# One decoder layer on one core: a 64-byte padding tile ahead of the activations in SBUF is left out

## The chip, the core and the metric

The kernel runs on one core of a Trainium2 chip. Its time is the device time of an execution in microseconds, and the figure compared is the median of several executions. A profile of one execution shows TensorE (PE, with its weight loads as PEld), VectorE (DVE), ScalarE (ACT), GpSimd (POOL), and the queue that issues most DMAs (SP).

## The reference

One layer of a hybrid decoder: two mixers side by side (differential attention and chunked retention) share an input and an output projection, and a gated MLP with a short causal convolution follows. 16 meta tokens stand ahead of 256 tokens; all is float32.

```python
u = rmsnorm(h, attn_norm) * vmask
proj = u @ w_in                              # 2048 -> 6144
aq, ak, av, rq, rk, rv, rg = jnp.split(proj, SPLITS, axis=-1)
ya = rmsnorm(diff_attention(aq, ak, av, lam, slopes, valid), attn_subln) * (1.0 - lam_init)
yr = rmsnorm(retention(rq, rk, rv, log_g), ret_norm) * silu(rg)
h = h + concat([ya, yr]) @ w_out             # 2048 -> 2048
u = rmsnorm(h, ffn_norm) * vmask
g = u @ w_gate                               # 2048 -> 5632
gc = causal_conv3(g, conv_w)
h = h + (silu(gc) * (u @ w_up)) @ w_down     # 5632 -> 2048
out = rmsnorm(h, final_norm)[:, CHUNK:]
```

## The kernel before

Every weight is used once, so the kernel is a stream over 212 chunks of 1 MB: 48 for the input projection (4 of them as `w_first`), 16 for `w_out`, 44 pairs for gate and up, 44 for `w_down`. `load` brings a chunk into `raw` by a DMA on SP, and `prep` (L118 to L131) splits each half of it into two parts of TensorE's fp32r type: ScalarE copies it into `whi` (L127), VectorE subtracts that from the original into `wlo` (L128). The activations are split in the same way into a high and a low part, and a product is three matmuls per 128 rows: high by high, high by low, low by high.

Four products follow one another on TensorE, each with a shape of its own:

- Input projection, `gemm` (L332 to L334): the weights are the stationary operand, `x` is the moving one, 258 or 272 columns. The attention and retention tasks are slipped in between.
- `w_out`, `gemm_q` on `ys` (L340 to L342): weights stationary, `ys` moving, 260, 256 and 258 columns. `ys` is the mixers' output, one row of `GW` = 544 float32 (2,176 bytes) for each of 16 steps k; the columns read begin at 28, 32 and 30 of that row (112, 128 and 120 bytes).
- Gate and up, on `g`, the normed input of the MLP, in the same layout as `ys`: `gemm_q` again for the gate (the same three lines), and `gemm_t` for the up product (L353, 512 columns that begin at byte 128 of a row; L355 or L352, 256 columns).
- Down, `down` (L709 to L711): here the activations are stationary. `fhi` and `flo` hold the MLP's 5,632 inner values as 44 rows of 256 tokens (1,024 bytes each); a matmul loads 128 of them (512 bytes) and streams 512 columns of `whi` or `wlo`. At the very end 72 matmuls of 256 columns (tile `oe`) take the place of 36 of 512.

A tile scheduler orders the instructions of each engine when the program is built. SBUF is laid out by pools, in the order in which they are opened: constants, `big`, the weights' `wts`, then `small` (statistics of a few bytes, each in a slot of 32 bytes or more), and above it the pools of the phases. The tile `spad`, [128, 16] float32, is 64 bytes in each partition and the first of `small`. Nothing reads it. In the built program the first bytes of a partition's tiles stand so:

| tile | first byte | past a multiple of 512 |
|---|---|---|
| `x` and later `g` (two tiles each, pool `big`) | 27,136 and 45,568 | 0 and 0 |
| `whi`, `wlo` (three buffers each) | 104,960 to 125,440 | 0 |
| `spad` | 129,536 | 0 |
| `ys`, later `fhi` | 130,624 | 64 |
| `flo` | 175,680 | 64 |

Of the kernel before, what the change touches and what calls it, by code (L numbers as in the profile page):

```python
# [10 lines left out]
F32 = mybir.dt.float32  # L11
# [8 lines left out]
P = 128  # L20
# [59 lines left out]
def trunk_kernel(ctx, tc, a, out):  # L80
    nc = tc.nc
    V, S, PE = nc.vector, nc.scalar, nc.tensor
# [2 lines left out]
    big = ctx.enter_context(tc.tile_pool(name="big", bufs=1))  # L85
    wp = ctx.enter_context(tc.tile_pool(name="wts", bufs=1))
    sp = ctx.enter_context(tc.tile_pool(name="small", bufs=2))
    spad = sp.tile([P, 16], F32, name="spad", bufs=1)
    V.memset(spad, 0.0)
    dp = ctx.enter_context(tc.tile_pool(name="dram", bufs=1, space=bass.MemoryType.DRAM))  # L90

    xs = [big.tile([P, 2, HK, TW], F32R, tag=f"act{i}", name=f"x{i}") for i in range(2)]
# [759 lines left out]
def build(arrs):  # L852
    import concourse.bacc as _bacc
    import concourse.tile as _tile
    from concourse import mybir as _mybir

    nc = _bacc.Bacc("TRN2", target_bir_lowering=False, num_devices=1)
    arrays, args = {}, {}
    for name, v in arrs.items():
        arrays[f"in_{name}_dram"] = v  # L860
        args[name] = nc.dram_tensor(f"in_{name}_dram", v.shape, _mybir.dt.from_np(v.dtype),
                                    kind="ExternalInput").ap()
    o = nc.dram_tensor("out_0_dram", (SEQ, D), _mybir.dt.from_np(np.dtype("float32")),
                       kind="ExternalOutput").ap()
    with _tile.TileContext(nc, schedule_with_timeline_sim=True) as tc:
        trunk_kernel(tc, args, o)
    return nc, arrays
# [8 lines left out]
```

## Time and profile before

| | |
|---|---|
| median of 3 executions | 1178.18 us (1177.35 to 1180.27) |
| the profiled execution | 1177.78 us, of which the span from first to last instruction is 1176.0 us |
| granted TensorE clock | 0.998 |
| PE busy, PEld busy | 1162.5 us (99%), 1079.7 us (92%) |
| DVE busy, ACT busy | 813.7 us (69%), 560.1 us (48%) |
| DMA | 224.42 MB, mean 191 GB/s |

A matmul's duration in the profile includes the time in which its results drain, which overlaps the next matmul; what a matmul costs on a busy TensorE is the distance from its start to the next start, called its pitch here. A row of the timeline begins with the start in us and the duration in us; an "x2" merges two instructions that follow each other. A row of a tile's view has the durations in ns as least/median/most.

### The profile page before, as it was taken

The page shows a single profiled execution, that of the slowest core. Times are in us where ns is not written, and L with a number is a line of the kernel's source. Part 1 is how long each engine was busy: PE and PEld are TensorE (multiplying, and loading weights), DVE is VectorE, ACT ScalarE, POOL GpSimd, SP SyncE. Part 2 cuts the span into 40 slices and gives each one's busy share as a digit, 9 for nine tenths or more (in the row PEclk, how much of TensorE's full clock was granted, in tenths as well). Part 3 has the DMA queues.
Part 4 walks back from the last instruction along what each step waited for, and adds up shares of the span by engine and source line. Part 5 has one row for each costly group of instructions (what it writes and reads, how often), then busy time and mean ns, then how long its engine had stood idle before and what let it go on. Part 6 is the DMA issues. An engine that isn't in the chain of part 4 may idle for free.

```text
span 1176.0 us, 20164 instructions
## 1 busy us (share of the span) xinstructions
PE 1162.5 (99%) x8039; PEld 1079.7 (92%) x8039; DVE 813.7 (69%) x1528; ACT 560.1 (48%) x922; POOL 3.7 (0%) x23
## 2 busy tenths in 40 slices
PE   9999999999999999999999999999999999999997
PEld 7999999999999999999999999999999888888886
DVE  7888887766677778777777777767777645454544
ACT  7666665443345444444444444444444434343442
POOL 0000000000000000000000000000000000000000
PEclk9999999999999999999999999999999999999999
DMA  8644545465557786555555555555555655555552
GB/s 300 210 157 163 186 149 182 160 191 177 179 184 232 228 268 222 179 182 190 198 183 180 188 197 189 180 184 195 196 179 183 225 198 182 181 192 198 181 182 105
DMA packets 76525, 224.42 MB, mean 191 GB/s; under 512 B 41362, under 2 KB 48954, under 8 KB 51472
## 3 DMA queue, kind: packets, MB, share of 16 engines
q1 hardware_dynamic: 76144, 221.96, 55.7%
q8 instruction: 63, 1.03, 0.3%
q0 software_dynamic: 144, 1.05, 0.2%
q14 instruction: 30, 0.25, 0.1%
q10 hardware_dynamic: 144, 0.14, 0.0%
HBM read 216.57 MB, written 6.55 MB: 190 GB/s over the span
## 4 chain that ended last, share of the span: by engine, by line
PE 94%; DMA 3%; DVE 1%; issue 0%; ACT 0%; SPq 0%; DVEq 0%; ACTq 0%
PE mm L353 14%; PE mm L340 10%; PE mm L342 10%; PE mm L341 9%; PE mm L332 7%; PE mm L333 7%; PE mm L334 7%; PE o L709 7%; PE o L711 7%; PE o L710 7%; PE mm L355 7%; DMA raw<-in_w_in_dram 2%; PE po L461 1%; PE ro L518 1%; DMA rvt<-rhv 1%; DMA raw<-in_w_first_dram 1%
## 5 line engine op out<-in xcount | busy, mean ns | idle before, releaser
L128 DVE TENSOR_TENSOR wlo<-raw,whi 128x1024 fp32r<-128x1024 f32 x381 | 466.4, 1224 | 278.9 <-ACT whi L127 272.5
L127 ACT CAST whi<-raw 128x1024 fp32r<-128x1024 f32 x381 | 399.9, 1050 | 472.4 <-PE o L711 132.5
L353 PE MATMUL mm<-g,whi 128*128 128x512 f32 x704 | 249.1, 392 | 0.0
L332 PE MATMUL mm<-x,whi 128*128 128x272 f32 (+1 forms) x688 | 198.8, 289 | 0.0
L340 PE MATMUL mm<-g,whi 128*128 128x260 f32 x704 | 198.7, 282 | 0.0
L333 PE MATMUL mm<-x,whi 128*128 128x272 f32 (+1 forms) x688 | 198.5, 289 | 0.0
L334 PE MATMUL mm<-x,wlo 128*128 128x272 f32 (+1 forms) x688 | 197.1, 287 | 1.4 <-DVE wlo L128 1.4
L342 PE MATMUL mm<-g,wlo 128*128 128x258 f32 x704 | 198.1, 281 | 0.0
L341 PE MATMUL mm<-g,whi 128*128 128x256 f32 x704 | 194.9, 277 | 0.0
L355 PE MATMUL mm<-g,wlo 128*128 128x256 f32 x660 | 185.1, 281 | 0.0
L353 PEld LDWEIGHTS mm<-g,whi 128*128 128x128 f32 x704 | 132.2, 188 | 25.9
L341 PEld LDWEIGHTS mm<-g,whi 128*128 128x128 f32 x704 | 133.5, 190 | 1.9
L340 PEld LDWEIGHTS mm<-g,whi 128*128 128x128 f32 x704 | 132.1, 188 | 0.0
L342 PEld LDWEIGHTS mm<-g,wlo 128*128 128x128 f32 x704 | 132.0, 187 | 0.0
L711 PE MATMUL o<-whi,flo 128*128 128x512 f32 x334 | 131.6, 394 | 0.0
L710 PE MATMUL o<-wlo,fhi 128*128 128x512 f32 x334 | 131.6, 394 | 0.0
L334 PEld LDWEIGHTS mm<-x,wlo 128*128 128x128 f32 x688 | 129.6, 189 | 1.7 <-DVE wlo L128 1.6
L333 PEld LDWEIGHTS mm<-x,whi 128*128 128x128 f32 x688 | 129.7, 189 | 0.0
L332 PEld LDWEIGHTS mm<-x,whi 128*128 128x128 f32 x688 | 129.7, 188 | 0.0
L355 PEld LDWEIGHTS mm<-g,wlo 128*128 128x128 f32 x660 | 124.3, 188 | 0.0
L709 PE MATMUL o<-whi,fhi 128*128 128x512 f32 x334 | 118.9, 394 | 0.0
L711 PEld LDWEIGHTS o<-whi,flo 128*128 128x128 f32 x334 | 62.5, 187 | 15.4
(244 smaller groups left out, 1372.7 us busy)
## 6 DMA issues: line engine op xcount, KB each, us to landing
raw<-in_w_in_dram SPq DMA_DIRECT2D x44, 1024.0 KB
raw<-in_w_gate_dram SPq DMA_DIRECT2D x44, 1024.0 KB
raw<-in_w_up_dram SPq DMA_DIRECT2D x44, 1024.0 KB
raw<-in_w_down_dram SPq DMA_DIRECT2D x44, 1024.0 KB
raw<-in_w_out_dram SPq DMA_DIRECT2D x16, 1024.0 KB
raw<-in_w_first_dram SPq DMA_DIRECT2D x6, 512.0 KB
xres<-in_x_dram SPq DMA_DIRECT2D x16, 129.0 KB
hd<-hb SPq DMA_DIRECT2D x64, 32.0 KB
```

The lines of the kernel that those rows point to most:

```text
L127: S.copy(out=hi, in_=src)
L128: V.tensor_tensor(out=lo, in0=src, in1=hi.bitcast(F32), op=ALU.subtract)
L332: PE.matmul(ps[:, :n], wh, xh, start=(k == 0), stop=False)
L333: PE.matmul(ps[:, :n], wh, xl, start=False, stop=False)
L334: PE.matmul(ps[:, :n], wl, xh, start=False, stop=(k == KT - 1))
L340: PE.matmul(ps[:, :NQ + 2], wh, src.cols(k, GO - 2, GL), start=(k == 0), stop=False)
L341: PE.matmul(ps[:, 4:NQ + 2], wh, src.cols(k, GL, GW), start=False, stop=False)
L342: PE.matmul(ps[:, 2:NQ + 2], wl, src.hi(k), start=False, stop=(k == KT - 1))
L353: PE.matmul(ps, wh, src.cols(k, GO + 2, GW), start=(k == 0), stop=(k == KT - 1))
L355: PE.matmul(ps[:, :SEQ], wl, src.cols(k, GO + 2, GL), start=False, stop=False)
L710: PE.matmul(o, ah, wl, start=False, stop=False)
L711: PE.matmul(o, al, wh, start=False, stop=stop and kk == 1)
```

## The change

`spad` and the instruction that clears it are left out. Every tile of the pools that lie above it moves down by 64 bytes in each partition: the rest of `small`, `ys` (to 130,560), `fhi` (130,560), `flo` (175,616), and all working tiles of the attention, retention, and MLP phases (`q2`, `k2`, `at`, `vt`, `fg`, `fs` and others). 130,560 and 175,616 are multiples of 512. The constants, `x`, `g`, `klz`, `htok`, `raw`, `whi` and `wlo` lie below and stay. The order of the instructions on each engine is the same but for the one that is gone; all lines below it have numbers smaller by 2.

```diff
     sp = ctx.enter_context(tc.tile_pool(name="small", bufs=2))
-    spad = sp.tile([P, 16], F32, name="spad", bufs=1)
-    V.memset(spad, 0.0)
     dp = ctx.enter_context(tc.tile_pool(name="dram", bufs=1, space=bass.MemoryType.DRAM))
```

## The prediction

> **What bounds the kernel now.** I read the page first (busy shares, then the chain that ended last), then the busy time by stretch, then who waits for TensorE, and last single rows of the timeline in the two stages that the moved tiles feed.
>
> ```profile
> PE 1162.5 (99%) x8039; PEld 1079.7 (92%) x8039; DVE 813.7 (69%) x1528; ACT 560.1 (48%) x922; POOL 3.7 (0%) x23
> PE 94%; DMA 3%; DVE 1%; issue 0%; ACT 0%; SPq 0%; DVEq 0%; ACTq 0%
> ```
>
> TensorE is busy for 99% of the span, and 94% of the chain that ended last is its own work. By stretch (length, then busy time and count of PE, PEld, DVE, ACT, POOL, the granted clock, DMA):
>
> ```profile
> 350.00:424.00 74.00, 74.00 (x622) 74.00 (x621) 55.84 (x107) 37.56 (x68) 0.00 (x0) 1.00 0.79 239
> 925.00:1148.00 223.00, 223.00 (x957) 178.73 (x956) 108.11 (x98) 90.31 (x96) 0.65 (x1) 1.00 0.55 191
> 500.00:900.00 400.00, 400.00 (x2843) 375.62 (x2842) 290.11 (x464) 183.01 (x285) 0.00 (x0) 1.00 0.54 187
> ```
>
> The first stretch is `w_out`, the second the down product, the third gate and up. TensorE never pauses in them, at full clock, while DVE and ACT have room. So in these stages nothing but the pitch of the matmuls makes time, and a change of addresses can only act through that pitch.
>
> Does the pitch depend on the address at all? The trace has a controlled pair: `gemm_q` runs with the same three shapes on `ys` and on `g`, both rows of 2,176 bytes, with the weights in the same buffers. Only the first byte differs: `ys` begins 64 past a multiple of 512, `g` on one. From the timeline, the first and last of 49 rows on `ys`, then on `g` (48 pitches, so 16 steps of three, each time):
>
> ```profile
> 399.80 0.28 PE L340 MATMUL mm<-ys,whi 128*128 128x260 f32 x1
> ...
> 405.53 0.28 PE L340 MATMUL mm<-ys,whi 128*128 128x260 f32 x1
> ```
>
> ```profile
> 606.97 0.28 PE L340 MATMUL mm<-g,whi 128*128 128x260 f32 x1
> ...
> 612.63 0.39 PE L353 MATMUL mm<-g,whi 128*128 128x512 f32 x1
> 612.87 0.28 PE L355 MATMUL mm<-g,wlo 128*128 128x256 f32 x1
> ```
>
> On `ys` the 48 take 5.73 us (358.1 ns for three), on `g` 5.66 us (353.8 ns). And the durations by tile:
>
> ```profile
> L340 PE MATMUL mm<-ys,whi x256: 277/284/291, 334.9 to 426.3; 128*128 128x260 f32 x128
> L341 PE MATMUL mm<-ys,whi x256: 276/279/287, 335.1 to 426.4; 128*128 128x256 f32 x128
> L340 PE MATMUL mm<-g,whi x704: 277/282/470, 426.7 to 915.8; 128*128 128x260 f32 x176
> L341 PE MATMUL mm<-g,whi x704: 274/278/281, 426.8 to 915.9; 128*128 128x256 f32 x176
> ```
>
> A row of 2,176 bytes is 4 x 512 + 128, so from k to k+1 the first byte steps by 128 in the 512, and each tile visits four positions. On `ys` the spread is 276 to 287 ns for one shape, on `g` 274 to 281. The timeline shows that on `ys` every fourth step is the slow one:
>
> ```profile
> 400.51 0.29 PE L340 MATMUL mm<-ys,whi 128*128 128x260 f32 x1
> 400.64 0.29 PE L341 MATMUL mm<-ys,whi 128*128 128x256 f32 x1
> ...
> 401.94 0.29 PE L340 MATMUL mm<-ys,whi 128*128 128x260 f32 x1
> 402.07 0.29 PE L341 MATMUL mm<-ys,whi 128*128 128x256 f32 x1
> ```
>
> So the address does act, through its place within 512 bytes, by one to three per cent of a matmul.
>
> **The change part by part.** *The instruction that goes.*
>
> ```profile
> 0.85 0.07 DVE L89 MEMSET spad<- 128x16 f32 x1
> 0.90 0.17 DVE L160 MEMSET ones<- 128x128 f32 x1
> 1.62 3.11 PE L178 MATMUL psx<-warm 128*128 128x512 bf16 x7 [1.62 <-DVE warm L166]
> 5.02 0.81 PE L231 MATMUL mm<-x,whi 128*128 128x258 f32 x4 [0.28 <-ACT x L213]
> ```
>
> The clears behind it start 0.05 us sooner (0.85 for 0.90), and with them the seven warm-up matmuls, which wait for `warm`. The first real matmul waits for ACT at 5.02, so this is covered: 0. No DMA is added, removed or moved past another, and no wait changes.
>
> *`w_out`.* After the change `ys` begins on a multiple of 512, with the layout of `g`: the 16 steps read from exactly the positions within 512 that the gate product reads today. I take the pitch of `g`: 16 chunks x (5.66 - 5.73) us = -1.1 us. Bounds: 0, if the difference comes from what runs beside it, and -1.2 us (to the rounding of these rows).
>
> *The down product.* Between these two rows of the chain of waits lie 80 repeats of 2.80 us, twelve matmuls each:
>
> ```profile
> 924.65 0.47 PE o L709 x2
> 1148.65 0.47 PE o L709 x2
> ```
>
> That is 224.00 us for 960 matmuls of 512 columns, 233.3 ns each. In all there are 1,020 of these (334 of each line, and 18 from the last tiles) and 72 of 256 columns. What changes is the stationary side: each slice of `fhi` and `flo` begins 64 past a multiple of 512 now, and on it afterwards. The moving side (`whi`, `wlo`) stays on multiples of 512. No down row has both on 512; the nearest is the up product, with weights on 512 and `g` 0, 128, 256 or 384 past it:
>
> ```profile
> L353 PE MATMUL mm<-g,whi x704: 388/393/398, 432.0 to 921.5; 128*128 128x512 f32 x176
> L709 PE MATMUL o<-whi,fhi x334: 388/394/398, 921.7 to 1157.8; 128*128 128x512 f32 x167
> L709 PEld LDWEIGHTS o<-whi,fhi x334: 187/187/192, 921.5 to 1157.6; 128*128 128x128 f32 x167
> L353 PEld LDWEIGHTS mm<-g,whi x704: 187/188/190, 431.9 to 921.3; 128*128 128x128 f32 x176
> 601.39 0.39 PE L353 MATMUL mm<-g,whi 128*128 128x512 f32 x1
> ```
>
> From 601.39 to the gate's first row at 606.97 the 16 pairs of 512 and 256 columns take 5.58 us, 348.8 ns a pair. At the down product's rate per column (233.3 / 512) a pair would take 350.0 ns. So both sides on 512 run 0.35% faster per column, 0.8 ns of 233.3, and x 1,020 that is -0.8 us. By the median durations of L353 and L709 (393 and 394) it would be -1.0 us; I take -0.9. The fast bound is the least duration of L709, 388 for 394: -6 ns x 1,020 = -6.1 us. The slow bound is what 64 bytes do to the moving side on `ys`, 287 for 279 in L341: +8 ns x 1,020 = +8.2 us; in the middle lies the most of L709, 398 for 394, +4.1 us. The weight load itself takes 187 ns at the median from an address 64 past (L709), as long as the 188 ns from one on 512 (L353), so its own duration gives no gain.
>
> *The rest.* The attention matmuls that read moved tiles are short and few:
>
> ```profile
> L461 PE MATMUL po<-vt,at x96: 270/272/303, 78.9 to 206.5; 100*86 100x128 f32 x48, 86*86 86x128 f32 x48
> L411 PE MATMUL sc<-k,q x48: 207/252/371, 55.6 to 193.5; 128*86 128x100 f32 x16, 128*86 128x186 f32 x16, 128*86 128x272 f32 x16
> ```
>
> These 144, and as many again for what the rows leave out, at the 2 ns by which the medians of L340 above differ, are 0.6 us either way; I take 0. The moved tiles that DVE and ACT write and read are not on the path: in the rows below the idle time of TensorE ahead of its groups (behind the bar, second) is 0.0 in the stages at issue.
>
> ```profile
> L711 PE MATMUL o<-whi,flo 128*128 128x512 f32 x334 | 131.6, 394 | 0.0
> L340 PE MATMUL mm<-ys,whi 128*128 128x260 f32 x256 | 72.3, 284 | 0.0
> ```
>
> The sum: 0 - 1.1 - 0.9 = -2.0 us. The profiled execution took 1177.78 us, 1.78 beyond its span, and 0.40 below the median of 1178.18, so it would take 1175.8 and the median 1176.2 us. A measurement of this kernel tells about 0.3%, 3.5 us, from no change; -2.0 is inside.
>
> [...]
>
> **The rivals.** *A: the down product falls toward its floor.* The weight load for the next matmul starts as the present one starts, so both streams run side by side, and the present 64 bytes between them could be a poor distance. For it: at the same distance of 64 bytes the pitch isn't fixed by the shape, since 256 columns there take
>
> ```profile
> 1163.07 0.28 PE L710 MATMUL oe<-wlo,fhi 128*128 128x256 f32 x1
> ...
> 1164.43 0.28 PE L710 MATMUL oe<-tailt,fhi 128*128 128x256 f32 x1
> ```
>
> 1.36 us for twelve, 113.3 ns, so twice that, 226.7, is possible for 512, 6.7 ns below today's. Against it: L353 reaches 388 only at its least. Half to all of the fast bound gives -3 to -6.1 us, with `w_out` -4.1 to -7.2: 1171 to 1174 us, 1172.5 in the middle.
>
> *B: the two streams collide when both begin on the same byte of 512.* They start together, and reading the same part of SBUF at once could hold one of them up. For it: those 113.3 ns, at a distance of 64, are below what 256 columns cost in the up product with both sides at distances of 0 to 384 (a third of 348.8, 116 ns, by columns). Price: from +4 ns (the most of L709 over its median) to +8 ns (L341 on `ys`) a matmul, +4.1 to +8.2 us, less `w_out`'s 1.1; it decides from +4.5 ns a matmul, where the sum passes +3.5 us. Its middle, +6 ns, gives +6.1 - 1.1 = +5.0 us, 1183 us. Against it: L353, whose every fourth step has both on 512, has no slow group (398 at most, as L709 has).
>
> *C: nothing happens.* `ys` is slower for what runs beside it (DMA at 0.79 there, 0.54 in gate and up), and the distance in the down product is indifferent: 1178.2 us. Against it stands the slow fourth step, which no neighbour's work would repeat so evenly.
>
> **How the numbers follow.** The forecast 0.36, C 0.10, A 0.34, B 0.20. The forecast is ahead of A because it has a stage with both sides on multiples of 128 and the weights on 512, timed over hundreds of matmuls, where A has only the short ones of the end. The first two fall within 0.3%: 0.46; A is faster, 0.34; B is slower, 0.20. The range reaches from 1170.5 (all of A's -7.2, and the 0.6 us of the short matmuls) to 1182 (B at +4 ns with no gain in `w_out`); the upper half of B is left out. The forecast's own range is 1174.7 to 1178.2, where no change begins.
>
> **What would show it.** In the profile after, 48 `gemm_q` pitches on `ys` take 5.66 us and no fourth step stands out; if 5.73 stays, C is right. Twelve matmuls of the down product take 2.79 us; 2.72 would be A, 2.85 or more B. Gate, up and input projection must keep their pitches. I am wrong if the pitch depends on something other than the place within 512 bytes.

## The result, and the profile after

The median went from 1178.18 us to 1172.66 us (seven executions each, 1170.49 to 1174.53 after), a ratio of 0.9946 with a 95% interval of 0.9931 to 0.9961: 5.5 us faster, about half a per cent. The profiled execution has a span of 1170.9 us, 5.1 us less. Times below leave out one slow execution, of the kernel called rows128 here, which took 1255.13 us at a granted clock of 0.85.

From the page of the kernel after, the busy times, the matmuls of 512 columns of the up product, and the largest matmul group of the down product (line numbers are smaller by 2):

```profile
PE 1156.8 (99%) x8039; PEld 1081.4 (92%) x8039; DVE 813.6 (69%) x1527; ACT 560.7 (48%) x922; POOL 3.7 (0%) x23
L351 PE MATMUL mm<-g,whi 128*128 128x512 f32 x704 | 249.1, 392 | 0.0
L709 PE MATMUL o<-whi,flo 128*128 128x512 f32 x334 | 130.0, 389 | 0.0
```

TensorE has the same matmuls and is still busy for 99%; the mean of a down matmul fell from 394 to 389 ns, that of the up product stayed at 392. The chain of waits after: the first, second and last of rows that stand twelve matmuls apart, as quoted for before:

```profile
925.85 0.45 PE o L707 x2
928.57 0.45 PE o L707 x2
...
1143.45 0.45 PE o L707 x2
```

From 925.85 to 1143.45 are 217.60 us for 80 repeats, 2.72 us for twelve, against 2.80. The pitch is 226.7 ns, 6.67 ns less than before. By tile, for the stationary side (its load first), the end of the down product (the row before, of L709, stands ahead of the row after, of L707), and `ys`:

```profile
L707 PEld LDWEIGHTS o<-whi,fhi x334: 187/188/192, 922.7 to 1152.4; 128*128 128x128 f32 x167
L707 PE MATMUL o<-whi,fhi x334: 389/389/396, 922.9 to 1152.6; 128*128 128x512 f32 x167
L709 PE MATMUL oe<-whi,fhi x12: 276/281/283, 1151.5 to 1165.6; 128*128 128x256 f32 x12
L707 PE MATMUL oe<-whi,fhi x12: 278/283/287, 1146.2 to 1160.3; 128*128 128x256 f32 x12
L338 PE MATMUL mm<-ys,whi x256: 277/282/285, 337.4 to 427.6; 128*128 128x260 f32 x128
L339 PE MATMUL mm<-ys,whi x256: 274/278/290, 337.5 to 427.7; 128*128 128x256 f32 x128
```

The weight load takes as long as before (188 for 187 ns at the median): nothing about the load itself is quicker. The stream `whi` has not moved by a byte. Yet the matmul that streams it while the load runs is shorter (389 for 394 ns at the median), so it is the two together that cost less. The 256-column matmuls of the end went the other way, from 281 to 283 ns at the median. On `ys` the slow fourth step is gone (285 at the most in L338, for 291), and 48 pitches, first and last row:

```profile
399.68 0.28 PE L338 MATMUL mm<-ys,whi 128*128 128x260 f32 x1
...
405.33 0.28 PE L338 MATMUL mm<-ys,whi 128*128 128x260 f32 x1
```

take 5.65 us, close to the 5.66 on `g`. Stage lengths, each from the start of a stage's first matmul to that of the next stage's, in us:

| stage | before, three profiles | after, three profiles | difference of the means |
|---|---|---|---|
| input projection, attention, retention | 333.31, 334.05, 333.12 | 335.78, 334.86, 335.65 | +1.94 |
| `w_out` | 91.74, 91.76, 91.76 | 90.57, 90.57, 90.57 | -1.18 |
| gate and up | 495.01, 495.01, 495.01 | 494.99, 494.99, 494.99 | -0.02 |
| down, to the last matmul's start | 246.14, 246.14, 246.14 | 239.80, 239.80, 239.80 | -6.34 |

The sum is -5.60 us, what the medians say. The last three stages repeat to 0.02 us; the first does not, and part of its growth is the granted clock, as the last experiments show. (The second and third profile of each kernel come from the runs below.)

### The profile page after: what moved, and what is told of

The parts are those of the page before. It is cut to its first block, busy times and chain, and to the rows that moved or that the text cites. A ratio compares the mean times of both kernels' runs of the same rounds, so it can differ in the third digit from the quotient of the medians.

```text
span 1170.9 us, 20163 instructions
## 1 busy us (share of the span) xinstructions
PE 1156.8 (99%) x8039; PEld 1081.4 (92%) x8039; DVE 813.6 (69%) x1527; ACT 560.7 (48%) x922; POOL 3.7 (0%) x23
## 4 chain that ended last, share of the span: by engine, by line
PE 93%; DMA 5%; DVE 2%; SPq 0%; issue 0%; ACT 0%; DVEq 0%; ACTq 0%
PE mm L351 14%; PE mm L340 10%; PE mm L338 10%; PE mm L339 9%; PE mm L353 7%; PE o L707 7%; PE o L709 7%; PE o L708 7%; PE mm L331 6%; PE mm L330 6%; PE mm L332 6%; DMA raw<-in_w_first_dram 2%; DMA rvt<-rhv 1%; PE po L459 1%; DMA raw<-in_w_in_dram 1%; PE ro L516 1%
## 5 line engine op out<-in xcount | busy, mean ns | idle before, releaser
L338 PE MATMUL mm<-g,whi 128*128 128x260 f32 x704 | 198.7, 282 | 0.0
L353 PE MATMUL mm<-g,wlo 128*128 128x256 f32 x660 | 185.1, 281 | 0.0
L338 PEld LDWEIGHTS mm<-g,whi 128*128 128x128 f32 x704 | 132.1, 188 | 0.0
L709 PE MATMUL o<-whi,flo 128*128 128x512 f32 x334 | 130.0, 389 | 0.0
L353 PEld LDWEIGHTS mm<-g,wlo 128*128 128x128 f32 x660 | 124.3, 188 | 0.0
L707 PE MATMUL o<-whi,fhi 128*128 128x512 f32 x334 | 117.1, 389 | 0.0
L709 PEld LDWEIGHTS o<-whi,flo 128*128 128x128 f32 x334 | 62.7, 188 | 13.0
```

Source lines behind the costliest of these rows:

```text
L338: PE.matmul(ps[:, :NQ + 2], wh, src.cols(k, GO - 2, GL), start=(k == 0), stop=False)
L353: PE.matmul(ps[:, :SEQ], wl, src.cols(k, GO + 2, GL), start=False, stop=False)
L709: PE.matmul(o, al, wh, start=False, stop=stop and kk == 1)
```

## The experiments

All kernels are the changed one with the edit shown. "48 on ys" and "twelve" stand for those pitches, read as above.

**Which part gives the time: padding back ahead of `ys` alone, or of `fhi` and `flo` alone.**

```diff
+        ypad = yp.tile([P, 16], F32, name="ypad")
+        V.memset(ypad, 0.0)
         ys = Packed([yp.tile([P, KT, GW], F32R, name="ys")])
```

> 64 bytes of padding stand ahead of ys alone: ys and the attention and retention tiles are back at their places of before, fhi and flo stay on multiples of 512. Theory (the gain is the down product's stationary side): twelve down matmuls take 2.72 us, 48 matmuls on ys 5.73 us, and the time is 6 us under before, ratio 0.9945 to 0.9955. Rival (the gain comes from ys and the tiles beside it): down at 2.80 us per twelve, ratio 0.998 or more.

```diff
+        fpad = fp.tile([P, 16], F32, name="fpad")
+        V.memset(fpad, 0.0)
         fhi = fp.tile([P, NF, SEQ], F32R, name="fhi")
```

> 64 bytes of padding stand ahead of fhi and flo alone; ys is on a multiple of 512. Theory (down's stationary side): twelve down matmuls take 2.80 us again, 48 matmuls on ys 5.66 us, and only w_out's 1.2 us of the gain is left, ratio 0.998 to 1.001. Rival (ys and its neighbours carry the gain): 1172 to 1174 us, ratio 0.995 to 0.997.

With `ys` at its old place: 1172.48 us beside 1178.92, ratio 0.9943 (0.9929 to 0.9958). `w_out` takes 91.76 us, as before, down 239.80, as after. With `fhi` and `flo` at theirs: 1177.73 us, ratio 0.9985 (0.9973 to 0.9998), `w_out` 90.57, down 246.14. From the chain of waits and by tile, the second kernel:

```profile
927.79 0.47 PE o L709 x2
930.59 0.47 PE o L709 x2
L709 PE MATMUL o<-whi,fhi x334: 387/395/398, 924.8 to 1161.0; 128*128 128x512 f32 x167
```

Twelve take 2.80 us again. So 64 bytes under the stationary side of the down product carry the gain, and `w_out` its 1.2 us. Both runs go the theory's way, and the rival's numbers fit neither.

**Distance or absolute place: padding ahead of the weights too.** Now `whi` and `wlo` lie 64 past a multiple of 512 as well as `ys`, `fhi` and `flo`; only `g` and `x` stay.

```diff
     wp = ctx.enter_context(tc.tile_pool(name="wts", bufs=1))
+    wpad = wp.tile([P, 16], F32, name="wpad")
+    V.memset(wpad, 0.0)
```

> 64 bytes of padding stand ahead of the weights: raw, whi, wlo, ys, fhi and flo all begin 64 past a multiple of 512, x and g on one. Theory (the distance between the streamed and the loaded operand within 512 bytes decides): twelve down matmuls at distance 0 take 2.72 us, ys against whi at the old distance of the gate product 5.66 us for 48, and gate, up and input projection change their pitch, since their distance is now 64 less. Rival (the absolute place decides, a loaded slice must begin on 512): down at 2.80 us, ys at 5.73 us, and gate and up slower by the 3% of a 512-column matmul, some 7 us.

1172.46 us, ratio 0.9944 (0.9927 to 0.9962). From the chain of waits:

```profile
925.55 0.45 PE o L709 x2
928.27 0.45 PE o L709 x2
```

```profile
L340 PE MATMUL mm<-ys,whi x256: 277/282/286, 335.9 to 426.0; 128*128 128x260 f32 x128
L353 PE MATMUL mm<-g,whi x704: 389/397/398, 431.8 to 922.4; 128*128 128x512 f32 x176
```

Nothing in the down product begins on a multiple of 512, except for its last tiles, and twelve take 2.72 us. `ys` also has its good pitch, 64 past, since `whi` is too. What changed for the worse is gate and up, 496.23 us for 494.99: `g` is on 512 and the weights are not (L353's median 397 for 393). So it is the distance between the loaded and the streamed operand. The price of it on gate and up was 1.2 us, far from the 7 that the rival named. The last tiles agree: `tailt` and `endt` stayed on multiples of 512 while `fhi` and `flo` lie 64 past, and twelve matmuls of 256 columns that stream `tailt` take 1.36 us here, as before the change, and 1.44 in the changed kernel (1158.45 to 1159.81, and 1158.66 to 1160.10).

**A map of the distance.** The rows of `fhi` and `flo` are put into one tile, in eight groups of six, with a gap between groups (`GAP` = 16 float32, 64 bytes; then 4, 16 bytes), so that one execution has eight distances. `ul` has one buffer for two, to make room. The diff leaves out the lines that write and read the rows through `row`.

```diff
+        fhl = fp.tile([P, 2 * NF * SEQ + 7 * GAP], F32R, name="fhl")
+        def row(lo, f, b=0, n=SEQ):
+            g = f // 6
+            s = g * (12 * SEQ + GAP) + lo * (6 if g < 7 else 2) * SEQ + f % 6 * SEQ + b
+            return fhl[:, s:s + n]
...
```

> fhi and flo lie in eight groups of six rows (the last of two), each group 64 bytes further from the last multiple of 512: 0, 64, 128 to 448, so that one run shows the down pitch at eight distances (one buffer less for the tile ul, which gate and up may feel a little). Theory (distance): 226.7 ns in the group at 0, 233.3 at 64, and a value of its own for each other distance, repeated in the four passes over the 44 rows. Rival (only a start on 512 is special): 226.7 at 0 and 233.3 in the seven others. Rival (no dependence on the place, the new pitch has another cause): one pitch in all groups.

> As the map in steps of 64, with eight groups that begin 0, 16, 32 to 112 bytes past a multiple of 512. Theory (distance decides, and 64 bytes is already a bad one): 226.7 ns at 0, rising to the 233 of 64 within a few steps, back toward 232 at 112. Rival (only a start on a whole 64-byte or larger unit matters): all steps between 0 and 64 alike.

From the chain of waits of the first map, twelve matmuls apart in its second pass over the rows, from the groups at 64, 192 and 256 bytes:

```profile
993.50 0.47 PE o L713 x2
996.30 0.47 PE o L713 x2
...
1007.47 0.47 PE o L713 x2
1010.22 0.45 PE o L713 x2
...
1018.45 0.45 PE o L713 x2
1021.17 0.45 PE o L713 x2
```

2.80, 2.75 and 2.72 us. The mean pitch of each group in that pass, from the time that its 36 matmuls take (12 in the last group), in ns:

| bytes past 512 | 0 | 64 | 128 | 192 | 256 | 320 | 384 | 448 |
|---|---|---|---|---|---|---|---|---|
| pitch | 227.2 | 233.3 | 232.4 | 229.1 | 227.2 | 233.3 | 232.4 | 229.7 |

| bytes past 512 | 0 | 16 | 32 | 48 | 64 | 80 | 96 | 112 |
|---|---|---|---|---|---|---|---|---|
| pitch | 227.7 | 226.9 | 233.1 | 233.3 | 233.2 | 231.8 | 234.2 | 233.2 |

(A group's edge takes in some matmuls at a neighbour's distance.) Full passes repeat to 0.01 us a group. The period is 256 bytes, not 512: a group at 256 is as good as one at 0. The good place is narrow, 0 and 16 bytes; 32 already cost the 6 ns. The theory held on the first map, and both rivals fell: neither one pitch for all, nor seven alike. On the second the rival fell, since 16 and 32 bytes differ by 6 ns; the theory's way back toward 232 at 112 bytes did not come (233.2). The whole kernels took 1174.98 and 1175.93 us in one execution each.

**The same rule for the other products.** Rows of 576 float32 are 2,304 bytes, nine times 256, so that every step k reads from the same place within 256; they fit into the slot that `x` had. In the first kernel the columns begin where they did, in the second 32 later.

```diff
-GO = 30
-GW = 544
-GL = 288
+GO = 62          # the first kernel keeps 30, 544 and 288
+GW = 576
+GL = 320
+GR = 576
...
-        ys = Packed([yp.tile([P, KT, GW], F32R, name="ys")])
+        ys = Packed([yp.tile([P, KT, GR], F32R, name="ys")])
-        gs = Packed([big.tile([P, HK, GW], F32R, tag=f"act{i}", name=f"g{i}")
+        gs = Packed([big.tile([P, HK, GR], F32R, tag=f"act{i}", name=f"g{i}")
```

> The rows of ys and g are 576 float32 long for 544 (2,304 bytes, nine times 256), the columns begin where they did, so that every step reads from the same place within 256 bytes: 112, 128 and 120. Theory (distance within 256 bytes decides): each step of three takes the 350 ns that every second one takes now (354 on average), 48 on ys or g take 5.60 us, an up pair some 351 ns for 348.8; gate and up together 1 to 2 us shorter, w_out 1 us, total 2 to 3 us under the changed kernel. Rival (the place within 512, or the step between rows, decides): no change or slower.

> Rows of 576 float32 as in the kernel beside it, and the columns begin 32 later, so that every step reads from 240, 256 and 248 bytes, the up product from a multiple of 256. Theory (distance within 256 bytes decides): each step of three takes the 358 ns of the slower steps, 48 on ys or g take 5.73 us, an up pair 348 ns or, if the 512 columns reach the 226.7 of the down product, 344; gate and up together from 1 us shorter to 4 us longer, w_out 1 us longer than changed. Rival (absolute multiples are best for every product): gate and w_out both faster than in the changed kernel.

At 112, 128 and 120 bytes (rows128): 1174.73 us, ratio 0.9972 (0.9959 to 0.9985), slower than the changed kernel where the edit acts: gate and up 497.95 us for 494.99, `w_out` 91.04 for 90.57. At 240, 256 and 248: 1169.47 us, ratio 0.9923 (0.9904 to 0.9942), gate and up 493.31 and `w_out` 90.48. From the second kernel's timeline, the first rows of an up product, of the gate that follows, and of the next up product:

```profile
599.79 0.39 PE L352 MATMUL mm<-g,whi 128*128 128x512 f32 x1
...
605.33 0.28 PE L339 MATMUL mm<-g,whi 128*128 128x260 f32 x1
...
610.99 0.39 PE L352 MATMUL mm<-g,whi 128*128 128x512 f32 x1
```

11.20 us for the two, against 11.24 (5.58 and 5.66) before: 5.54 for up, 5.66 for the gate. The theory missed: both products went against its sign in the first kernel, and in the second gate and up gained more than its best and `w_out` gained where it should have lost. I had taken the times of single steps out of a sequence whose steps alternate, and added them up as if each kept its time among steps of its own kind; a step that took 350 ns beside one of 358 takes 356 (5.69 us for 16) alone. Whole products can be compared: 16 pairs of the up product take 5.54 us with every step on a multiple of 256, 5.62 with every step 128 past one (606.27 to 611.89 in the first kernel), and 5.58 in the mix of both. The rival, that multiples of 256 are best for every product, was right in sign, though the gain lies in the up product and `w_out` gained only 0.1 us. This kernel has the least time of the study, 2.9 us under the changed one measured beside it (1172.33); the stages that the edit reaches hold 1.8 of it.

**The changed kernel again, and the first stage.** The stage of the input projection was 2.5 us longer in the first profile after, which no term of mine held.

> The changed kernel once more, unaltered, beside the others of this call. Theory (w_out gives 1.2 us and the down product 6.3): 1170 to 1173 us, and the stages from w_out on as in its first profile to 0.1 us, while the input projection's stage, which waits for DMAs, differs by a microsecond or two. Rival (the 2.5 us that the input projection's stage was longer in the first profile after belong to the moved attention tiles): that stage is 335.5 us or more again.

> The kernel before, unaltered, for one more profile: how long is the input projection's stage (first matmul to the first on ys) from one execution to the next? Theory (its length follows DMA landings and not the place of the attention tiles): it varies over 333 to 338 us as among the kernels with moved tiles. Rival (the moved tiles make it longer): it stays at 333.3 to 333.7, as in the two profiles with the tiles at their old places.

> The kernel before a third time, for the same question, with the same expectations: 333 to 338 us by the theory, 333.3 to 333.7 by the rival.

> The changed kernel a third time: the input projection's stage at 333 to 338 us by the theory (two profiles gave 335.8 and 334.9), at 334.9 or more by the rival; all later stages as before to 0.1 us by both.

The first of these, timed: 1172.33 us beside 1178.09, ratio 0.9948 (0.993 to 0.9967). The stage lengths stand in the table above: 333.1 to 334.1 us before, 334.9 to 335.8 after. Neither the theory's 333 to 338 nor the rival's 333.3 to 333.7 is quite what the kernel before showed, and the 335.5 that the rival named for the changed kernel was missed by the first of these runs (334.86). Where it arises, by stretch (length; busy time and count of PE, PEld, DVE, ACT, POOL; clock, DMA), the late part of the stage before and after, and four microseconds of it:

```profile
240.00:312.00 72.00, 70.55 (x559) 69.37 (x559) 47.55 (x82) 25.54 (x31) 0.11 (x1) 1.00 0.57 179
296.00:300.00 4.00, 4.00 (x34) 4.00 (x34) 0.86 (x2) 1.62 (x4) 0.00 (x0) 1.00 0.19 76
```

```profile
240.00:312.00 72.00, 69.83 (x542) 68.55 (x541) 45.17 (x76) 25.29 (x31) 0.11 (x1) 0.98 0.54 167
296.00:300.00 4.00, 4.00 (x20) 3.81 (x19) 0.43 (x1) 1.07 (x3) 0.00 (x0) 0.57 0.24 100
```

17 matmuls fewer in the same 72 us, and 14 fewer in the four microseconds from 296 alone, in which TensorE is busy throughout: the clock granted there was 0.57 on average, for 1.00 before. In the timeline the matmuls of 272 columns start every 0.23 us up to 299.6 and every 0.125 us from there. The rest is idle time, 0.7 us more. Who TensorE waited for (total, times, longest), before and after:

```profile
PE ro L518 <- DMA rvt<-rhv: 1.4, 1, 1.4
PE mm L334 <- DVE wlo L128: 1.4, 1, 1.4
```

```profile
PE ro L516 <- DMA rvt<-rhv: 2.1, 1, 2.1
PE mm L332 <- DVE wlo L126: 1.7, 1, 1.7
```

It waits longer for a DMA of the retention's values, and the half clock begins 0.5 us behind that pause. The third profile after has such a stretch too, behind a pause of 2.1 us at 52:

```profile
52.00:55.50 3.50, 3.49 (x15) 3.50 (x16) 2.92 (x4) 0.00 (x0) 0.12 (x1) 0.51 0.50 89
```

The second profile after has none in this stage, and neither has any of the three before. A stretch of 3.4 us at half clock costs 1.7 us (an estimate: half its length). Without it the stage is 334.1, 334.9 and 333.9 us after, beside 333.3, 334.1 and 333.1: 0.8 us more on average, and no longer apart. So about 1.1 of the 1.94 us is this clock. A last kernel keeps all the good places and moves the attention and retention tiles alone back, by padding behind `ys`:

```diff
         ys = Packed([yp.tile([P, KT, GW], F32R, name="ys")])
+        ypad = yp.tile([P, 16], F32, name="ypad")
+        V.memset(ypad, 0.0)
```

> 64 bytes of padding stand behind ys: ys, fhi and flo are on multiples of 512 as in the changed kernel, and the attention and retention tiles at their places of before. Theory (the input projection's stage is 1.9 us longer in the changed kernel because these tiles moved): the stage takes 333.1 to 334.1 us, the time is 7 to 7.5 us under before, 1170.5 to 1171.5. Rival (it follows DMA landings or where ys is written): 334.9 us or more, and 1172 to 1173.

1170.83 us beside 1178.18, ratio 0.9940 (0.9926 to 0.9953); the stage takes 333.01 us, all later ones as after. These are about the theory's numbers, but they do not show it: this profile has no half clock in the stage, and the interval overlaps that of the changed kernel. Over all profiles, less 1.7 us for each 3.4 us at half clock, the stage takes 333.0 to 334.2 us with these tiles at their places of before within 512 bytes (the three of before, `ys` at its old place, the kernel with padding ahead of the weights, and this one), and 332.6 to 336.0 with them moved (the three after, the padding ahead of `fhi`, the two maps, and the two kernels with longer rows, where they lie 2,048 bytes above the changed kernel's). The two longest as measured, 337.89 us (rows128, 6.8 us at half clock) and 337.67 (the padding ahead of `fhi`, 3.4 us), owe much to the clock. That the moved tiles make the stage longer is not shown; what is left over, under a microsecond on average, stays open.

## Why the prediction was right or wrong

The time, 1172.66, lies in the range of 1170.5 to 1182, and next to the middle of rival A, 1172.5 by a down product at its floor. That it came so close is in part luck: A's middle has less than the whole fast bound, the down product fell by more than all of it, and the first stage took some of this back. The forecast of 1176.2, within 0.3% of before, was not what happened: the likeliest case was chosen wrongly, by a term that was too small.

- What bounds the kernel: right for the three later stages, which changed by TensorE's pitch alone. That the address acts through the place within 512 bytes was right in direction; the place that counts is the distance of the two operands within 256.
- `w_out`, -1.1 us: measured -1.18, and alike in every profile. The controlled pair, one product on two tiles, gave it to 0.1 us, since the changed kernel reads from the very positions of the row used.
- The down product, -0.9 us: the step that failed. Measured -6.34: the 1,020 matmuls of 512 columns gave -6.7 us (mean pitch over all of them 226.8 for 233.3 ns), and the 72 of 256 columns at the end cost +0.3 (119.6 for 114.8 ns). I had taken the rate of the up product, whose matmuls of 512 columns alternate with 256 and begin at four places within 512, for that of a sequence at one distance. Within 256 bytes these four are two, 0 and 128, and 128 is a bad one: 232.4 ns in the map for 227.2 at 0. So the 348.8 ns for a pair was a mean of good and bad steps, and the row with "both sides on 512" was not one. The fast bound, from the least duration of L709 (388), was the right row: the steady 389 is next to it, and twice 113.3 ns is the 226.7 measured.
- Rival B, a collision with both on 512: wrong for 512 columns. Its sign was right for the 256 columns of the end, where the pitch did rise by 4.8 ns on average. A's ground, that the 113.3 ns of the end could be had for 512 columns, named the right number although at the old distance; it was not the same cause.
- The cleared tile: 0 was right. `warm` is still waited for at 1.6 us.
- Attention and retention, 0 with 0.6 us either way: the stage grew by 1.94 us on average, three times that bound: some 1.1 us came from the half clock in two of the three profiles, and 0.8 is left, of which no cause is shown. The later stages alone, -7.5 us, would give 1170.7. Executions of the two kernels that recorded the same mean clock (0.995 to 0.999, over all runs) differ by 6.1 to 6.9 us on average, so that 5.5 us is rather the low end of what the change is worth.
- C, nothing happens: wrong. Only the address of the load was changed, and twelve matmuls of the down product went from 2.80 to 2.72 us: 233.3 and 226.7 ns for the same stream beside a load from two addresses.

## What to carry to other kernels

Where TensorE never pauses, compare the pitch of equal matmuls between tiles at different addresses before calling it given: here 64 bytes were 2.6% of a product (6.34 of 246.14 us). In a kernel like this one, try the streamed and the next loaded fp32r operand at the same place within 256 bytes (here 226.7 ns for 512 columns, for 233.3 at 64 bytes), with row lengths that are multiples of 256 bytes, so that every step has it, as the fastest kernel here does (1169.47 us); and check the pitch in the profile, since the short matmuls here, of 256 columns, took 120.0 ns at that place and 113.3 at 64 bytes. Do not price a uniform sequence by rows taken out of a mixed one: take the least and the most of those rows as bounds, and expect that a steady sequence can sit on one of them. Before a difference of a microsecond or two between profiles is put down to an edit, look at the granted clock by stretch: here 3.4 us at half clock made some 1.7 us (the estimate above).

## What the runs showed of the hardware

The pitch of 512 fp32r columns, with a 128-column weight load beside it, was 226.7 ns at a distance of 0 in the changed kernel (in the first map 227.2 at 0 and at 256 bytes, group edges included), 233.3 at 64 in the kernel before and in the map, and in the map 232.4 at 128 and 229.1 at 192. It depended on the distance and not on the address, in the one case tried: with both operands 64 bytes past 512 twelve took 2.72 us, too. The load's recorded duration at the median was 187 ns at 64 bytes (before) and 188 at 0 (after). Why the distance counts, and why with a period of 256 bytes, no run shows. The best distance was not the same for both shapes: at 64 bytes 256 columns took 113.3 ns (before) and 512 columns 233.3, the worst in the map of 64-byte steps; at a distance of 0 they took 120.0 (after) and 226.7.

A matmul's recorded duration was longer than its pitch, 389 ns for 226.7 at 512 columns and 283 for 120.0 at 256 in the changed kernel. What the last matmul there wrote was read 0.31 us behind its start (it starts at 1162.74, VectorE's instruction that waits for it at 1163.05), 0.03 us behind the end of its record.

In 5 of the 14 profiles the granted clock fell to half inside the first stage, for 3.4 us (6.8 in one); over the whole span it was 0.996 or 0.997 in these and 0.998 or 0.999 in the other nine. In the first profile after, the half clock began at 296.18, 0.5 us behind a pause of TensorE of 2.1 us; in the third it stood from 52.0, behind another of 2.1. In the second a pause of 2.1 us passed without it, so what decides is not shown.
